# 1/rms at attention's entry put on the products that give k, q and v, with tied logits pairs and later statistics transposes

## The chip, the cores and the metric

The kernel runs on one core of a Trainium2 chip. The metric is the device time of one launch in microseconds (us), as the median of several runs. A core has five engines that run their own queues in order and wait for one another by semaphores: TensorE (PE in the profile, its weight loads PEld), VectorE (DVE), ScalarE (ACT), GpSimd (POOL) and SyncE (SP), which here issues the transfers. Products are gathered in PSUM, eight banks of 512 float32 columns; everything else lies in SBUF.

## The reference, cut to what matters

A trunk of two layers on 1024 positions of width 1024 in float32. Layer 0 mixes by a short gated convolution, layer 1 by differential attention over k and v that are made from the residual stream after layer 0. In each layer a convolution FFN and a gated embedding of the layer (called ple here) follow, and RMS norms stand before and after every part.

```
def rms_norm(x, g):
    return x * rsqrt(mean(x * x, axis=-1) + 1e-6) * g

# layer 1: 8 heads, two maps of 64 each, values of 128
k, v = split(rms_norm(x, g_kv) @ w_kv)
q    = rms_norm(x, g_pre_mix[1]) @ w_q
for each block of 128 queries:
    logits = q . k * 64 ** -0.5 + bias(distance), causal
    probs  = softmax(logits)                        # of both maps, m = 0 and 1
    o      = (probs[m = 0] - lam * probs[m = 1]) @ v
o   = rms_norm(o, g_subln) * (1 - lambda_init)
x   = x + rms_norm(o @ w_o, g_post_mix[1])

# every layer
x   = x + rms_norm(conv_ffn(rms_norm(x, g_pre_ffn)), g_post_ffn)
x   = x + rms_norm(sigmoid(rms_norm(x, g_pre_ple) @ w_gate) * (p @ w_proj), g_post_ple)
```

## The kernel before, in words

Activations lie transposed, channels on the 128 partitions and 512 positions along the free axis. So a half (0 or 1) of the sequence is eight tiles of 128x512, and every stage runs for half 0 and then for half 1. A float32 value is used as two parts in the float32r format, `hi` (a cast, on ScalarE) and `lo` (the value less `hi`, on VectorE, `split`, L249 and L250), and a product takes three passes, hi.hi, lo.hi and hi.lo (`mm3`, L256 to L258). Weights come as 128x1024 pieces (`wr`), get their gain on POOL where the stage asks for it (L159), and are split into `wh` (L162) and `wl` (L165, two of three on VectorE and the third on POOL).

The program is a list of steps. A step loads and splits weights ahead, makes its products, and then gives the background work a number of ticks (`ticks`, two to four for most). The background is a queue of generators, and a tick runs the first of them to its next `yield`. A step's `need` names what must have been made before; where it has not, ticks are spent at once until it has. The order in which each engine gets its instructions is then fixed, before the run, by a planner that takes what it thinks is ready in the order of the program, by its own estimate of durations. On the chip each engine follows that order, ready or not.

The background work between two stages is `gen_post`. It takes the outputs y of a stage with the sum of their squares, `acc`, which has one partial sum for each partition, and makes 1/rms: `mean4` transposes `acc` on TensorE (L307) and sums over the free axis (L309); `rsqrt4` starts on VectorE and ends with ten small instructions on POOL (L291 to L300); `bcast4` spreads the result over the partitions by four transposes (L318) and a copy (L322), which gives `rb`. Then, for each of eight tiles k, y is scaled by it (L430, VectorE), added to x (L432, POOL), and x squared and summed into a new `acc` (L268 on ScalarE, L269 on VectorE). Before attention x is also stored to `xscr` in DRAM (`spill`) for the residual. From the new `acc` comes a second 1/rms by the same chain, and with it the inputs of the next stage: `make_h` multiplies x by `rb` (`hn`, L350) and splits it (L249, L250). In some places (`defer`, half 1 of ple) the inputs are made from x without its 1/rms, and the products of the stage take it on instead: the gates of half 1 are scaled out of PSUM at L710, followed by the sigmoid (L711) and the product with the embedding (L714).

At attention's entry stand, in this order, the eight gate steps of ple for half 1, then k and q of head 0 for half 0, two steps of v, and k and q of head 0 for half 1, ahead of the first attention unit. The k and q products go to the two PSUM tiles `pd` and leave them as `hi` with a factor on ScalarE (L834) and `lo` on VectorE (L835); v leaves by one copy (L865). Its products are those of L861.

Attention has 64 units, a head and a block of 128 queries each. A unit's `softmax` makes the logits of both maps, 64 rows of the array each (L962), three passes for each half of the keys, in the tiles `qk`. A block of the first half keeps both maps in one tile; a block of the second half needs a tile for each map, and there are two tiles in all. L969 adds the bias and takes the minimum of the negated logits, L972 the exponential, L975 to L978 join the maps. `transp` (L988) and `values` (L1003) follow two and three units later. The other projections ("dense" steps) are mixed in between units by `pace`.

## Time and profile before

| | |
|---|---|
| median of 3 runs | 2830.05 us (2828.73 to 2830.48) |
| the profiled execution | 2831.85 us, span 2830.1 us |
| granted TensorE clock, mean | 0.977 |
| busy: TensorE, VectorE, ScalarE, POOL | 2698.0, 1649.8, 1258.5, 815.8 us |

The span is the stretch between the first and the last instruction of one profiled execution; what lies around it is in that execution's own time. The busy times are sums over the span. A granted clock of 1 is 2.4 GHz and one of 0.5 is 1.2 GHz; a value between is a mean over a stretch.

### The profile page before, as it was taken

The numbers are of one execution on the slowest core, as the hardware profiler recorded it, in microseconds if no ns is written. First come the engines' busy times: TensorE is split into PE (matmuls) and PEld (weight loads), VectorE is DVE, ScalarE is ACT, GpSimd is POOL, SyncE is SP. The second block draws the span as 40 slices with busy tenths as digits, with TensorE's granted clock in tenths as the row PEclk, the third lists the DMA queues.
The fourth block names the chain that finished last, engine by engine and source line by source line (L and its number), as shares of the span: only waits on it lengthen the run. The fifth ranks groups of instructions, "written<-read, shape, count | busy, mean of one in ns | idle before, by whom it ended". The sixth has DMA issues, their size and how long they took to land.

```text
span 2830.1 us, 33443 instructions
## 1 busy us (share of the span) xinstructions
PE 2698.0 (95%) x12526; PEld 2186.8 (77%) x12526; DVE 1649.8 (58%) x2171; ACT 1258.5 (44%) x2034; POOL 815.8 (29%) x1037
## 2 busy tenths in 40 slices
PE   8999999999989999884999999998999999999996
PEld 7887877888868888763888888776888887888875
DVE  7446366555485555768554545428755558555577
ACT  5233344444454444533454545534544445444442
POOL 3223142221152211454223222225222115221134
PEclk9999999999999999996999999998999999999998
DMA  4222222222242232232111111352222222222242
GB/s 173 98 96 77 96 83 92 94 97 100 97 136 97 97 105 97 90 104 82 60 45 53 53 53 61 114 206 97 90 97 89 97 97 82 90 97 97 97 141 82
DMA packets 86515, 269.56 MB, mean 95 GB/s; under 512 B 9688, under 2 KB 12032, under 8 KB 86352
## 3 DMA queue, kind: packets, MB, share of 16 engines
q1 hardware_dynamic: 86352, 267.42, 27.8%
q8 instruction: 98, 1.61, 0.2%
q14 instruction: 65, 0.53, 0.1%
HBM read 247.42 MB, written 24.68 MB: 96 GB/s over the span
## 4 chain that ended last, share of the span: by engine, by line
PE 49%; DVE 6%; POOL 1%; issue 1%; ACT 1%; DVEq 0%; ACTq 0%; POOLq 0%
PE ps L257 7%; PE ps L258 7%; PE ps L256 7%; PE qk L962 4%; PE pd L861 3%; PE ps L645 3%; PE ps L644 3%; PE ps L646 3%; PE pd L256 3%; PE pd L257 3%; PE pd L258 3%; PE st L1003 2%; DVE hy L430 2%; PE st L988 1%; DVE acc L269 1%
## 5 line engine op out<-in xcount | busy, mean ns | idle before, releaser
L256 PE MATMUL ps<-hy,wh 128*128 128x512 f32 x1960 | 784.0, 400 | 15.7 <-ACT hy L333 7.5
L257 PE MATMUL ps<-hy,wl 128*128 128x512 f32 x1960 | 784.9, 401 | 14.8 <-DVE wl L165 14.8
L258 PE MATMUL ps<-hy,wh 128*128 128x512 f32 x1960 | 781.3, 399 | 0.0
L165 POOL TENSOR_TENSOR wl<-wr,wh 128x1024 fp32r<-128x1024 f32 x136 | 355.5, 2614 | 1009.3 <-ACT wh L162 997.8
L162 ACT CAST wh<-wr 128x1024 fp32r<-128x1024 f32 x412 | 432.7, 1051 | 321.7 <-PE ps L646 152.4
L257 PEld LDWEIGHTS ps<-hy,wl 128*128 128x128 f32 x1960 | 373.2, 190 | 108.8 <-DVE wl L165 18.3
L165 DVE TENSOR_TENSOR wl<-wr,wh 128x1024 fp32r<-128x1024 f32 x276 | 349.5, 1267 | 184.7 <-ACT wh L162 181.4
L256 PEld LDWEIGHTS ps<-hy,wh 128*128 128x128 f32 x1960 | 372.9, 190 | 108.3 <-ACT hy L333 7.9
L258 PEld LDWEIGHTS ps<-hy,wh 128*128 128x128 f32 x1960 | 372.5, 190 | 90.4 <-DVE hy L334 0.7
L502 DVE SCALAR_TENSOR_TENSOR c<-u,cst,c 128x512 f32<-128x512 f32 x192 | 149.5, 780 | 352.9 <-ACT c L501 348.1
L607 ACT COPY u<-ps 128x512 f32<-128x512 f32 x176 | 103.4, 587 | 409.3 <-PE ps L258 403.5
L644 PE MATMUL ps<-jit,wh 128*128 128x512 f32 x704 | 273.9, 389 | 0.0
L645 PE MATMUL ps<-jit,wl 128*128 128x512 f32 x704 | 273.9, 389 | 0.0
L646 PE MATMUL ps<-jit,wh 128*128 128x512 f32 x704 | 236.2, 389 | 0.0
L250 DVE TENSOR_TENSOR jit<-hid,jit 128x512 fp32r<-128x512 f32 x176 | 166.6, 959 | 95.7 <-ACT jit L249 95.6
L269 DVE TENSOR_TENSOR acc<-acc,sq 128x512 f32<-128x512 f32 x165 | 146.7, 891 | 114.3 <-ACT sq L268 111.0
L644 PEld LDWEIGHTS ps<-jit,wh 128*128 128x128 f32 x704 | 132.2, 188 | 27.6
L645 PEld LDWEIGHTS ps<-jit,wl 128*128 128x128 f32 x704 | 132.2, 188 | 27.4
L646 PEld LDWEIGHTS ps<-jit,wh 128*128 128x128 f32 x704 | 132.2, 188 | 27.4
L249 ACT CAST jit<-hid 128x512 fp32r<-128x512 f32 x176 | 109.4, 622 | 98.6 <-PE ps L646 90.8
L257 PE MATMUL ps<-s,wl 128*128 128x512 f32 (+1 forms) x368 | 143.3, 390 | 10.3 <-DVE wl L165 10.3
L503 DVE SCALAR_TENSOR_TENSOR c<-u,cst,c 128x512 f32<-128x512 f32 x192 | 146.7, 766 | 5.7
(159 smaller groups left out, 3828.5 us busy)
## 6 DMA issues: line engine op xcount, KB each, us to landing
wr<-w_ffn_up SPq DMA_DIRECT2D x176, 512.0 KB, 3.2
wr<-w_ffn_down SPq DMA_DIRECT2D x88, 512.0 KB, 3.2
wr<-w_sc_in SPq DMA_DIRECT2D x48, 512.0 KB, 3.2
wr<-w_ple_gate SPq DMA_DIRECT2D x32, 512.0 KB, 3.3
wr<-w_sc_out SPq DMA_DIRECT2D x16, 512.0 KB, 3.3
wr<-w_o SPq DMA_DIRECT2D x16, 512.0 KB, 3.7
oscr<-oh SPq DMA_DIRECT2D x28, 256.0 KB, 2.0
wr<-w_v SPq DMA_DIRECT2D x10, 512.0 KB, 3.3
```

The lines of the kernel that those rows point to most:

```text
L162: nc.scalar.copy(out=hi[:, :n], in_=raw[:, :n])
L165: eng.tensor_tensor(lo[:, :n], raw[:, :n], hi[:, :n].bitcast(F32), ALU.subtract)
L250: (lo_eng or nc.vector).tensor_tensor(dst_lo, src, dst_hi.bitcast(F32), ALU.subtract)
L256: nc.tensor.matmul(out, whi[:, c], hi, start=(i == 0), stop=False)
L257: nc.tensor.matmul(out, wlo[:, c], hi, start=False, stop=False)
L258: nc.tensor.matmul(out, whi[:, c], lo, start=False, stop=(i == n - 1))
L269: nc.vector.tensor_tensor(acc, acc, t, ALU.add)
L502: nc.vector.scalar_tensor_tensor(c, u_in[:, 1:HT + 1], cst[:, wcol + 1:wcol + 2], c, ALU.mult, ALU.add)
L503: nc.vector.scalar_tensor_tensor(c, u_in[:, 0:HT], cst[:, wcol:wcol + 1], c, ALU.mult, ALU.add)
L644: nc.tensor.matmul(o, hi[:, c], j[:, 0, :], start=(k == 0), stop=False)
L645: nc.tensor.matmul(o, lo[:, c], j[:, 0, :], start=False, stop=False)
L646: nc.tensor.matmul(o, hi[:, c], j[:, 1, :], start=False, stop=(k == NF - 1))
```

## The change

It does three things.

- ple of layer 0 now makes the inputs of k, q and v in the loop that updates x, as `split(hi, lo, xn)` without 1/rms. 1/rms of x is still made (`stat_keep`), and the steps of k, q and v need it: k and q are multiplied by its broadcast (and q by -0.125) on VectorE as they leave PSUM and then split, v by its column form on ScalarE, in two parts of 256 columns. The tile of x is given up after its store inside the loop, no longer after it. The broadcast lies in a third `rb`, no longer in `rk`.
- The logits of the two maps are issued in turn, map 1 first, and `tc.issue_after` ties each to come behind the one before in TensorE's queue. It is an order in that queue and no semaphore; other instructions may come between.
- `lag` puts two ticks before `mean4` and two before `bcast4`, and `behind` ties their transposes to come after the last product of `mm3` (or of the FFN's down step) issued so far.

The tile `oh` of the normed attention output has two buffers where it had three.

```diff
 LEAD = 6
 RATE = 0.75
+LAG_A = 2
+LAG_B = 2
...
         (lo_eng or nc.vector).tensor_tensor(dst_lo, src, dst_hi.bitcast(F32), ALU.subtract)
...
+    last_mm = [None]
+    def behind():
+        return tc.issue_after(last_mm[0]) if last_mm[0] is not None else nullcontext()
     def mm3(out, whi, wlo, pairs, kcols):
...
             nc.tensor.matmul(out, whi[:, c], hi, start=(i == 0), stop=False)
             nc.tensor.matmul(out, wlo[:, c], hi, start=False, stop=False)
-            nc.tensor.matmul(out, whi[:, c], lo, start=False, stop=(i == n - 1))
+            last_mm[0] = nc.tensor.matmul(out, whi[:, c], lo, start=False, stop=(i == n - 1)).ins
...
     def k128(i):
...
     def mean4(sq, nb=4):
...
         m = sb_()
-        for c in range(nb):
-            nc.tensor.transpose(m[:, k128(c)], sq[:, k128(c)], ident)
+        with behind():
+            for c in range(nb):
+                nc.tensor.transpose(m[:, k128(c)], sq[:, k128(c)], ident)
...
     def bcast4(r, keep=False, raw=False):
...
         b = sb_()
-        for c in range(r.shape[1]):
-            nc.tensor.transpose(b[:, k128(c)], r[:, c:c + 1].to_broadcast([P, P]), ident)
+        with behind():
+            for c in range(r.shape[1]):
+                nc.tensor.transpose(b[:, k128(c)], r[:, c:c + 1].to_broadcast([P, P]), ident)
         if raw:
             return b
-        rb = cur[0].tile([P, HT], F32, tag="rk", name=nm("rk"), bufs=2) if keep else wk("rb")
+        rb = cur[0].tile([P, HT], F32, tag="rk", name=nm("rk"), bufs=2) if keep else wk("rb", bufs=3)
...
         return rb
...
-    def stat_keep(sq, key):
+    def lag(n):
+        for _ in range(n):
+            yield
+    def stat_keep(sq, key, on=False):
+        yield from lag(LAG_A)
         v = mean4(sq)
         r = rsqrt4(v, True)
-        yield
-        have["r", key] = (bcast4(r, True), r)
+        yield from lag(LAG_B)
+        have["r", key] = (bcast4(r, not on), r)
...
     def make_hg(x, gname, k, hi, lo):
...
     def stat_r(sq):
+        yield from lag(LAG_A)
         v = mean4(sq)
         r = rsqrt4(v)
-        yield
+        yield from lag(LAG_B)
...
     def make_h(xs, rb, gname, key, alloc, drop=False):
...
         acc = None if last else wk("acc", bufs=3)
         new, hs = [], []
-        if defer:
+        if defer and not spill:
...
                     yield False
                 hi, lo = al(F32R), al(F32R)
-                make_hg(xn, gname, k, hi, lo)
+                if gname is None:
+                    split(hi, lo, xn)
+                else:
+                    make_hg(xn, gname, k, hi, lo)
+                if spill:
+                    hy.free(1)
...
             have[targets[0][1]] = hs
             slots_of[targets[0][1]] = al
-            yield from stat_keep(acc, targets[0][1])
+            yield from stat_keep(acc, targets[0][1], spill)
...
                 slots_of[key] = al
                 have["r", key] = have["r", targets[0][1]]
-            if spill:
-                hy.free(ND)
...
                         nc.tensor.matmul(o, hi[:, c], j[:, 0, :], start=(k == 0), stop=False)
                         nc.tensor.matmul(o, lo[:, c], j[:, 0, :], start=False, stop=False)
-                        nc.tensor.matmul(o, hi[:, c], j[:, 1, :], start=False, stop=(k == NF - 1))
+                        last_mm[0] = nc.tensor.matmul(o, hi[:, c], j[:, 1, :], start=False, stop=(k == NF - 1)).ins
...
                     have[f"y_ple{L}", half] = (ys, acc[0])
                     bg.append(gen_post(half, (f"y_ple{L}", half), f"post_ple{L}", targets, last=(L == 1),
-                                       spill=(L == 0)))
+                                       spill=(L == 0), defer=(L == 0)))
...
                 hi, lo = (pool.tile([P, HT], F32R, tag="kq", name=nm("kq"), bufs=KQ) for _ in range(2))
                 sc = -0.125 if isq else 1.0
-                nc.scalar.activation(hi, p_, AF.Copy, scale=sc)
-                nc.vector.scalar_tensor_tensor(lo, p_, sc, hi.bitcast(F32), ALU.mult, ALU.subtract)
+                t = wk("hn")
+                nc.vector.scalar_tensor_tensor(t, p_, sc, have["r", ("xn", half)][0], ALU.mult, ALU.mult)
+                split(hi, lo, t)
...
                 ensure(hy, 1)
                 v = hy()
-                nc.scalar.copy(out=v, in_=p_)
+                r = have["r", ("xn", half)][1]
+                for j in range(2):
+                    c = slice(j * 256, (j + 1) * 256)
+                    tb = (t2 % 2) * 2 + j
+                    nc.scalar.activation(v[:, c], p_[:, c], AF.Copy, scale=r[:, tb:tb + 1])
...
             w, g = kq(h, isq)
             for i, half in enumerate(halves):
-                step(kq_part(h, isq, half, hold), w if i == 0 or again else None, need=[("xn", half)], g=g,
+                step(kq_part(h, isq, half, hold), w if i == 0 or again else None, need=[("xn", half), ("r", ("xn", half))], g=g,
...
         def v_steps(g, hold, t2s, load):
...
                 step(v_first(hold), a["w_v"][g, 0], ticks=0, g=("kv", 0, 4))
             for i, t2 in enumerate(t2s):
-                step(v_part(g, t2, hold), a["w_v"][g, 1] if load and i == 0 else None, need=[("xn", t2 // 2)], g=("kv", 4, 4),
+                step(v_part(g, t2, hold), a["w_v"][g, 1] if load and i == 0 else None, need=[("xn", t2 // 2), ("r", ("xn", t2 // 2))], g=("kv", 4, 4),
...
                 lg = [ps_.tile([P, S], F32, tag="qk", name=nm("qk"), bufs=2) for _ in range(2)]
             q = qt[h, half]
+            prev = None
...
                 k = kt[h, c]
                 for i, (a_, b_) in enumerate(((0, 0), (0, 1), (1, 0))):
-                    for m in range(2):
+                    for m in (1, 0):
                         r = slice(64 * m, 64 * m + 64)
-                        nc.tensor.matmul(lg[m][:, c * HT:c * HT + ce], q[a_][r, k128(qb)], k[b_][r, 0:ce],
-                                         start=(i == 0), stop=(i == 2))
+                        with tc.issue_after(prev) if prev is not None else nullcontext():
+                            prev = nc.tensor.matmul(lg[m][:, c * HT:c * HT + ce], q[a_][r, k128(qb)], k[b_][r, 0:ce],
+                                                    start=(i == 0), stop=(i == 2)).ins
...
                 hi, lo = hy(F32R), hy(F32R)
             else:
-                hi, lo = (scopes["att"][1].tile([P, HT], F32R, tag="oh", name=nm("oh"), bufs=3) for _ in range(2))
+                hi, lo = (scopes["att"][1].tile([P, HT], F32R, tag="oh", name=nm("oh"), bufs=2) for _ in range(2))
...
             nc.vector.scalar_tensor_tensor(lo, p_, gsub, hi.bitcast(F32), ALU.mult, ALU.subtract)
             if h == NH - 1:
```

## Rows read from the trace of the kernel before

**Rows 1.** The page, busy time, share of the span and instructions of each engine.

```profile
PE 2698.0 (95%) x12526; PEld 2186.8 (77%) x12526; DVE 1649.8 (58%) x2171; ACT 1258.5 (44%) x2034; POOL 815.8 (29%) x1037
```

**Rows 2.** TensorE's waits, whole span: who waited for whom, total, times, longest.

```profile
PE st L307 <- DVE acc L269: 37.6, 7, 19.9
PE ps L257 <- DVE wl L165: 25.1, 12, 5.7
```

**Rows 3.** Stages: busy us of PE, PEld, DVE, ACT, POOL, then clock, DMA share.

```profile
1232.00:1247.00 15.00, 9.53 (x33) 6.94 (x33) 14.45 (x15) 6.63 (x10) 6.89 (x4) 0.89 0.44 154
...
1268.00:1288.00 20.00, 1.10 (x4) 0.60 (x4) 20.00 (x25) 9.34 (x16) 7.08 (x3) 0.57 0.28 100
1288.00:1316.00 28.00, 27.73 (x176) 24.12 (x174) 20.79 (x35) 11.57 (x23) 12.13 (x16) 0.94 0.16 58
1316.00:1341.00 25.00, 1.13 (x5) 0.73 (x5) 20.50 (x31) 8.41 (x17) 16.86 (x18) 0.56 0.30 105
...
1440.00:1560.00 120.00, 120.00 (x746) 100.12 (x744) 58.04 (x136) 55.41 (x126) 33.70 (x68) 1.00 0.15 49
```

**Rows 4.** Timeline around the first k product: start, duration, instruction, times, idle before.

```profile
1268.05 0.39 PE L258 MATMUL ps<-s,wh 128*128 128x512 f32 x1
...
1285.92 1.87 DVE L710 TENSOR_TENSOR hy<-ps,rk 128x512 f32<-128x512 f32 x3
...
1287.34 0.77 PE L256 MATMUL pd<-hy,wh 128*128 128x512 f32 x1 [18.90 <-ACT hy L711]
...
1290.12 3.07 DVE L269 TENSOR_TENSOR acc<-acc,sq 128x512 f32<-128x512 f32 x4
```

**Rows 5.** Timeline of half 1's statistics.

```profile
1307.15 0.56 ACT L322 COPY rb<-st 128x512 f32<-128x512 f32 x1
...
1309.81 11.49 DVE L430 SCALAR_TENSOR_TENSOR hy<-hy,cst,rb 128x512 f32<-128x512 f32 x8
...
1324.24 2.72 DVE L269 TENSOR_TENSOR acc<-acc,sq 128x512 f32<-128x512 f32 x1
...
1335.63 1.12 PE L307 MATMUL st<-ident,acc 128*128 128x128 f32 x4 [19.90 <-DVE acc L269]
1340.99 0.47 PE L318 MATMUL st<-ident,rs_r 128*128 128x128 f32 x1 [4.24 <-POOL rs_r L300]
...
1342.35 0.59 ACT L322 COPY rb<-st 128x512 f32<-128x512 f32 x1 [0.37 <-PE st L318]
...
1359.16 0.60 ACT L834 ACTIVATE kq<-pd 128x512 fp32r<-128x512 f32 x1 [5.12 <-PE pd L258]
```

**Rows 6.** Groups by line and shape: count, busy us, mean ns, idle before.

```profile
L250 DVE TENSOR_TENSOR hy<-hn,hy 128x512 fp32r<-128x512 f32 x76 | 59.9, 800 | 14.4 <-ACT hy L249 13.9
...
L835 DVE SCALAR_TENSOR_TENSOR kq<-pd,kq 128x512 fp32r<-128x512 f32 x32 | 22.0, 688 | 62.2 <-ACT kq L834 61.8
...
L969 DVE CUSTOM_DVE_ANT_0 s<-qk,T 128x1024 f32<-128x1024 f32 x16 | 19.3, 1222 | 1.2 <-PE qk L962 0.8
...
L350 DVE TENSOR_TENSOR hn<-hy,rb 128x512 f32<-128x512 f32 x16 | 12.4, 791 | 5.6 <-ACT rb L322 5.0
...
L710 DVE TENSOR_TENSOR hy<-ps,rk 128x512 f32<-128x512 f32 x13 | 8.6, 680 | 3.6 <-PE ps L258 3.6
```

**Rows 7.** TensorE's timeline, logits of four units (the first shape of a run stands).

```profile
1304.14 0.98 PE L962 MATMUL qk<-kq,kq 64*128 64x256 f32 x12
...
1307.83 1.49 PE L962 MATMUL qk<-kq,kq 64*128 64x384 f32 x12
...
1793.60 1.31 PE L962 MATMUL qk<-kq,kq 64*128 64x512 f32 x6
```

**Rows 8.** Busy time of L962 alone over attention (TensorE, weight loads, clock, DMA).

```profile
1300.00:1840.00 540.00, 109.55 (x576) 72.18 (x576) 0.97 0.19 65
```

**Rows 9.** TensorE's waits for acc from 340 to 1240, and from 1860 to 2740.

```profile
PE st L307 <- DVE acc L269: 12.1, 3, 7.8
...
PE st L307 <- DVE acc L269: 3.5, 2, 2.9
```

More of the change, by code (lines that the diff above doesn't have):

```diff
@@ L2 @@
 from collections import deque
-from contextlib import ExitStack
+from contextlib import ExitStack, nullcontext
 import concourse.bass as bass
@@ L754, in finish @@
             if c == 0:
-                rs = wk("rb")[:, 0:256]
+                rs = wk("rb", bufs=3)[:, 0:256]
                 nc.scalar.copy(out=rs, in_=rb[:, 0:256])
```

## The prediction

> **What bounds the kernel now.** I read the page first: TensorE is busy for 2698.0 us of the span, so an edit counts only where it shortens TensorE's own work or closes one of its gaps [rows 1]. Second, the waits of TensorE, to see which gaps a named producer ends: 37.6 us in seven waits of the statistics transposes L307 for `acc`, 25.1 us in twelve for the lower half of a weight (`wl`), and one of 18.9 us before the first `pd` product [rows 2, 4]. Third, the stages, to tell which engine each is bound by. Around attention's entry TensorE works 1.10 us of the 20 from 1268 and 1.13 us of the 25 from 1316, while VectorE works 20.00 and 20.50 us of them; the granted clock is 0.57 and 0.56 there, so part of those stretches is at 1.2 GHz. In attention proper TensorE works 120.00 of 120.00 us, VectorE 58.04 and ScalarE 55.41 [rows 3]. So the entry is bound by VectorE and the statistics chain, attention by TensorE. What VectorE or ScalarE does in attention is under cover; what TensorE does there is paid in full.
>
> **What the entry waits for.** For half 0, the multiplication by 1/rms (`hn`, L350) and the split (L250) stand in VectorE's queue between the last gates' L710 and L714: the last three L710 run at 1285.92, and the first k product starts at 1287.34, 19 us after the last gate product at 1268.05. The last gates' y is not summed before 1293.2 (L269) [rows 4]. For half 1 the chain of statistics runs twice: from that sum to the broadcast of 1/rms, copied at 1307.15; then eight L430 (11.49 us), the adds on POOL, the sum over x, and L307 at 1335.63, where TensorE has stood 19.90 us; 4.24 us more until 1/rms is back at 1340.99 for L318; only then eight `hn` and eight splits. k of half 1 leaves PSUM at 1359.16 [rows 5].
>
> **The parts, with their cost.**
>
> *Entry.* Removed: 16 `hn` of 791 ns, 12.4 us of VectorE [rows 6]. Moved: 16 pairs of a cast on ScalarE and a split L250 (800 ns) into the loop that updates x, so that k and q need x and not its statistics. The 16 stores to `xscr` are issued where they were, SyncE's queue keeps its order; only the tile is given up sooner. Added: each k and q product is scaled by VectorE out of PSUM (nearest row L710, also PSUM times SBUF, 680 ns), then cast, then split (800), where one scaled copy on ScalarE and L835 (688) did it [rows 6]: about 0.8 us more of VectorE for each of 32, 25 us, under TensorE's 120 of 120 us [rows 3]. Each v leaves in two copies of half width in place of one, on ScalarE, under the same cover. Without that cover the 25 us would be paid: that is rival B.
>
> What is late next is 1/rms of half 1, now needed where k of half 1 leaves PSUM. Behind that multiplication on VectorE stand the softmax minima (L969) and the next `wl`; behind the two `pd` banks stand v, k and q of everything later. When does it come? Without the eight `hn` of half 0 in its way, the last gate's y is summed soon after the last gate product ends (1268.4): L710, sigmoid, L714, square and L269 at 0.6 to 0.8 each, 3.5 us, so 1272 in place of 1293.2 [rows 4]. From there to the copied broadcast took 14 us: 1286. From L430's start to L307 took 25.8 us (1309.8 to 1335.6), with softmax work between; eight splits come in (6.4 us at 0.80, or 11.5 at the 1.44 that an L430 costs beside POOL's adds), and some softmax work can stand elsewhere: I take 28, so 1315. From L307 to the copied broadcast took 7.3 us (1335.63 to 1342.94) [rows 5, 6]: 1323. Meanwhile TensorE has four steps of half 0 and the first units' logits (27.7 us as from 1288 to 1316 [rows 3], of which some 5 are logits, so 5.6 a step), then two steps for k and q of half 1 (11.2) and a few us of the first units' transposes: 42 us from 1268, to 1310. So a wait of some 13 us stays where 43 stood (18.9, 19.9 and 4.2). k of half 1 leaves PSUM at about 1324 in place of 1359, 35 us sooner; the wait that stays leaves the clock low for some us after it, for which I take off 5. **Entry: 30 us**, between 5 (the broadcast is about as late as before, or the splits delay the weights at 1232 to 1247, where VectorE is busy for 14.45 of 15 us [rows 3]) and 45 (no wait left: 43, and the clock).
>
> The Trainium skill speaks against the move (SBUF — State Buffer, "Who interferes with whom"): a VectorE instruction with two SBUF inputs contends with a GpSimd instruction that reads SBUF. The splits have two such inputs and move beside POOL's adds, so by that rule all 16 cost near 1.44 us and the entry would give some 20 to 25 us, not 30; the trace agrees in kind, with an L269 of 2.72 us beside POOL's work and four in 3.07 us elsewhere.
>
> *Tied logits pairs.* The two maps of a head use 64 rows of the array each. Where their products alternate, twelve run in 0.98 us (256 columns) and twelve in 1.49 us (384 and 512, 5,376 columns); where one map's six run alone, they take 1.31 us for 2,304 columns, half of that unit [rows 7]. All 576 keep TensorE busy for 109.55 us [rows 8]. The first four blocks of a head, whose two maps share one tile, already alternate: 0.98 + 1.49 = 2.47 us for each of 8 heads, 19.8 us. The other 32 units have 89.8. They hold 20,736 columns a head (by the code's widths); at the alternating rate (1.49 us for 5,376) that is 5.75 us a head, 46 in all, so 44 us is the most that tying gives, and nothing the least. I take 35: some units alternate already in part, other instructions may come between tied ones, and a pair waits for the later of two tiles. TensorE has no idle time in these stages [rows 3], so its saving is the kernel's.
>
> *Later statistics transposes.* Two ticks before each of the two transposes put L307 and L318 about one step (5.6 us) later in TensorE's queue. Outside entry and end L307 waits 12.1 us before the entry, 7.8 of them at once, and 3.5 us after attention [rows 9]. The 7.8 us is about a step and a half, so most of it should go; for the shorter waits I count nothing, since the tick moves the producer's queue with it. The transposes themselves cost the same. **5 us**, between -8 (the L430 runs shift onto other weights' `wl` waits) and 15 (all of it).
>
> *Nothing:* `oh` with one tile less (its stores have four units, some 28 us, until the next half); the third `rb` (two are held through attention by the halves' 1/rms, and the one left serves the posts there, one at a time).
>
> Sum: 30 + 35 + 5 = 70. The profiled execution took 2831.85 us (span 2830.1), 1.8 above the median of the runs; 2831.85 - 70 = 2761.9, less 1.8 is **2760**.
>
> **Rivals.**
>
> A. *The wait for 1/rms takes the place of the one removed.* k and q of half 1 hold both `pd` banks until the broadcast; if POOL's weight work stands before the ten small rsqrt steps and VectorE's queue holds the sum over x back, the chain keeps its old end. Against: 21 us of the old delay (1272 to 1293.2) is VectorE's backlog at the gates, which goes. Then the entry gives 3: 2787.
>
> B. *Shorter logits don't shorten attention*, because leaving PSUM and softmax set the pace. For: VectorE now scales k and q too. Against: VectorE 58 and ScalarE 55 of 120 us. The pairs then give nothing: 2795. The Trainium skill has this as a rule (TensorEngine Tiling (Array Packing), "PSUM Bottleneck"): tiling speeds TensorE but not the evacuation, which may become the limit.
>
> C. *Slower.* A tied pair waits for the later tile, which the unit before frees only after both its minima (L969, 1.22 us each at 1024 columns [rows 6], behind a queue). Today TensorE starts the first map meanwhile. If the planner places the pair too early, TensorE stands in order behind it. With 32 such units this overtakes the whole gain at 2.2 us a unit (70/32); at 3 us, 96 - 70 gives 2856. Against: L962 is in none of the larger waits of TensorE today, and dense products fill the gaps.
>
> D. *No change:* the order comes out so that each gain is given back elsewhere (the `wl` waits of 25.1 us double, entry as in A): 2830.
>
> **How the numbers follow.** Forecast 0.60 (own range 2738 to 2785), A 0.15, B 0.11, C 0.10, D 0.04. This kernel's measurement tells 0.2% (5.7 us) from no change. Faster: forecast, A and B, 0.86; within 0.2%: D, 0.04; slower: C, 0.10. The range takes in forecast, A and B: from 2734 (entry 42, pairs 42, transposes 12, near their upper ends) to 2800; C and D are left out.
>
> **What would show it.** Right: no gap of TensorE of 19 us between the last gate and the first k; no L350; L962 busy for near 75 us in 576 instructions; L307's waits under 15 us in all. Wrong: a `pd` wait for VectorE's scaling of k of over 25 us; L962 among TensorE's large waits; VectorE busy throughout the entry as before.

## The result and the profile after

The changed kernel takes **2798.24 us** (median of 4, 2797.49 to 2799.38) beside 2830.12 us of the kernel before on the same chip: a ratio of 0.9887 [0.9874, 0.9899], 32 us or 1.1% faster. The forecast was a gain of 70 us. The profiled execution took 2797.83 us (span 2796.0). Two kernels further below had one execution each in a slow state, of 4360.21 and 2938.4 us; their medians are those of the other runs.

New line numbers: mm3 L264 to L266, transposes of the statistics L316 and L328, their sum L318, ten 1/rms steps on POOL L299 to L308, copy of the broadcast L332, gains of weights on POOL L161, `wl` L167, split L252, square and sum L276 and L277, y scaled L446 and added L448, the gates L729, L730 and L733, scaling of k and q L854, v's products L881 and its copies out of PSUM L889, logits L988.

The page's first part and TensorE's longest waits stand against [rows 1, 2].

```profile
PE 2676.2 (96%) x12526; PEld 2168.2 (78%) x12526; DVE 1676.6 (60%) x2187; ACT 1258.1 (45%) x2050; POOL 820.2 (29%) x1037
```

```profile
PE ps L265 <- DVE wl L167: 27.0, 11, 6.3
PE st L328 <- POOL rs_k L308: 23.9, 3, 13.0
PE st L316 <- DVE acc L277: 12.6, 7, 3.3
...
PE pd L266 <- DVE hy L252: 8.3, 3, 5.4
```

The wait of 18.9 us for the gates' last step ahead of the first k product is gone, and the waits for `acc` fell from 37.6 to 12.6 us. A new one has come: 23.9 us for `rs_k`, the end of the ten small steps on POOL. TensorE's own work fell by 21.8 us.

Both kernels issue 12,526 instructions on TensorE, so the start of the n-th shows where time was won (us; the last two columns are experiments below, and the traced execution of the last one took 2756.84 us, the fastest of its kernel):

```
n-th start       before    after    difference   1/rms on VectorE   all three repairs
5000 (ahead)     1194.4   1191.2       -3.2            1192.0            1191.0
5750 (entry)     1394.9   1380.4      -14.5            1370.6            1359.6
8500 (after)     1857.0   1824.9      -32.1            1815.1            1784.2
12526 (last)     2821.0   2787.3      -33.7            2778.3            2746.3
```

Of the 34 us some 3 were won ahead of the entry, 11 in it, 18 in attention and 2 behind it. The entry, by stages as in [rows 3] (the third window is 29 us long, to where TensorE runs on):

```profile
1268.00:1288.00 20.00, 12.66 (x53) 10.39 (x54) 13.26 (x17) 5.82 (x9) 11.56 (x14) 0.83 0.39 133
1288.00:1316.00 28.00, 18.59 (x134) 15.88 (x133) 24.73 (x32) 13.61 (x28) 23.32 (x21) 0.87 0.28 105
1316.00:1345.00 29.00, 14.36 (x54) 10.07 (x53) 18.68 (x30) 9.07 (x18) 12.57 (x15) 0.74 0.20 73
...
1440.00:1560.00 120.00, 120.00 (x771) 98.49 (x771) 71.39 (x157) 58.25 (x135) 38.44 (x82) 1.00 0.16 54
```

TensorE is busy for 45.61 of these first 77 us, where it worked 29.96 of 73 in [rows 3]. In attention proper it stays at 120.00 of 120.00 while VectorE rises from 58.04 to 71.39: the scaling moved there is under cover, as forecast.

Where TensorE stands now, from its timeline (answers to [rows 4, 5]):

```profile
1266.90 0.40 PE L266 MATMUL ps<-s,wh 128*128 128x512 f32 x1
1275.34 1.12 PE L328 MATMUL st<-ident,rs_k 128*128 128x128 f32 x4 [8.04 <-POOL rs_k L308]
1276.10 0.78 PE L264 MATMUL pd<-hy,wh 128*128 128x512 f32 x1
...
1329.84 0.66 PE L316 MATMUL st<-ident,acc 128*128 128x128 f32 x4 [1.37 <-DVE acc L277]
1343.48 0.47 PE L328 MATMUL st<-ident,rs_k 128*128 128x128 f32 x1 [12.98 <-POOL rs_k L308]
```

And what the two long waits wait for, on POOL:

```profile
1268.45 0.20 POOL L299 TENSOR_TENSOR rs_t<-rs_k 128x4 f32<-128x4 f32 x1 [5.25 <-DVE rs_k L287]
1269.35 2.50 POOL L161 TENSOR_TENSOR wr<-wr,cst 128x1024 f32<-128x1024 f32 x1 [0.69 <-DMA wr<-w_v]
1271.81 0.65 POOL L300 TENSOR_TENSOR rs_t<-rs_t,rs_v 128x4 f32<-128x4 f32 x1
...
1275.08 0.20 POOL L308 TENSOR_TENSOR rs_k<-rs_k,rs_t 128x4 f32<-128x4 f32 x1
...
1335.01 0.20 POOL L299 TENSOR_TENSOR rs_t<-rs_k 128x4 f32<-128x4 f32 x1 [1.65 <-DVE rs_k L287]
1335.29 0.20 POOL L300 TENSOR_TENSOR rs_t<-rs_t,rs_v 128x4 f32<-128x4 f32 x1
...
1338.21 1.90 POOL L161 TENSOR_TENSOR wr<-wr,cst 128x1024 f32<-128x1024 f32 x1 [2.15 <-DMA wr<-w_k]
1340.06 0.20 POOL L303 TENSOR_TENSOR rs_t<-rs_k 128x4 f32<-128x4 f32 x1
1340.21 1.90 POOL L161 TENSOR_TENSOR wr<-wr,cst 128x1024 f32<-128x1024 f32 x1
...
1343.22 0.20 POOL L308 TENSOR_TENSOR rs_k<-rs_k,rs_t 128x4 f32<-128x4 f32 x1
```

Ten steps of 0.2 us, issued 0.28 us apart where nothing is between them, would take 2.8 us. They take 6.8 and 8.4 here, because gains of weights stand between them in POOL's order, and these wait for the transfers of the weights (0.69 and 2.15 us) and then run for 1.9 to 2.5 us. VectorE and ScalarE show the rest of both chains, and what the first costs y of half 1:

```profile
1266.62 0.68 DVE L318 TENSOR_REDUCE rs_v<-st 128x4 f32<-128x512 f32 x1
...
1276.49 0.59 ACT L332 COPY rb<-st 128x512 f32<-128x512 f32 x1 [2.49 <-PE st L328]
1276.97 0.64 ACT L730 ACTIVATE hy<-hy 128x512 f32<-128x512 f32 x1
1277.64 2.38 DVE L733 TENSOR_TENSOR hy<-hy,s 128x512 f32<-128x512 f32 x1 [3.25 <-ACT hy L730]
1280.72 0.69 DVE L277 TENSOR_TENSOR acc<-acc,sq 128x512 f32<-128x512 f32 x1 [0.70 <-ACT sq L276]
...
1331.14 3.30 DVE L167 TENSOR_TENSOR wl<-wr,wh 128x1024 fp32r<-128x1024 f32 x1
...
1344.84 0.59 ACT L332 COPY rb<-st 128x512 f32<-128x512 f32 x1 [0.37 <-PE st L328]
1345.46 1.29 DVE L854 SCALAR_TENSOR_TENSOR hn<-pd,rb 128x512 f32<-128x512 f32 x2 [10.54 <-ACT rb L332]
```

The last gate's sigmoid (L730) stands on ScalarE behind the copy of `rb`, which waits for that same 1/rms. So y of half 1 is summed at 1281.4, where the forecast had 1272. POOL is not alone in this: the sum of half 0's statistics (L318) starts on VectorE 7.5 us after its transposes have ended (1259.1), behind the work of the last gates and a `wl`, and in half 1's chain a `wl` of 3.30 us (1331.14) stands on VectorE ahead of the steps for POOL.

### The profile page after: what moved, and what is told of

Read it like the earlier page. It is cut to its first block, busy times and chain, and to the rows that moved or that the text cites. A ratio compares the mean times of both kernels' runs of the same rounds, so it can differ in the third digit from the quotient of the medians.

```text
span 2796.0 us, 33415 instructions
## 1 busy us (share of the span) xinstructions
PE 2676.2 (96%) x12526; PEld 2168.2 (78%) x12526; DVE 1676.6 (60%) x2187; ACT 1258.1 (45%) x2050; POOL 820.2 (29%) x1037
## 4 chain that ended last, share of the span: by engine, by line
PE 47%; DVE 6%; POOL 2%; issue 1%; ACT 1%; DMA 0%; DVEq 0%; SPq 0%; POOLq 0%; ACTq 0%
PE ps L265 7%; PE ps L264 7%; PE ps L266 7%; PE pd L881 3%; PE ps L665 3%; PE ps L663 3%; PE ps L664 3%; PE qk L988 3%; PE pd L264 2%; PE pd L266 2%; PE pd L265 2%; PE st L1029 2%; DVE hy L446 1%; PE st L1014 1%; DVE acc L277 1%
## 5 line engine op out<-in xcount | busy, mean ns | idle before, releaser
L264 PE MATMUL ps<-hy,wh 128*128 128x512 f32 x1960 | 783.2, 400 | 16.4 <-ACT hy L348 8.3
L266 PE MATMUL ps<-hy,wh 128*128 128x512 f32 x1960 | 781.6, 399 | 0.0
L167 POOL TENSOR_TENSOR wl<-wr,wh 128x1024 fp32r<-128x1024 f32 x136 | 355.1, 2611 | 1007.1 <-ACT wh L164 997.8
L264 PEld LDWEIGHTS ps<-hy,wh 128*128 128x128 f32 x1960 | 373.1, 190 | 107.4 <-ACT hy L348 8.6
L266 PEld LDWEIGHTS ps<-hy,wh 128*128 128x128 f32 x1960 | 372.5, 190 | 90.3 <-DVE hy L349 0.8
L167 DVE TENSOR_TENSOR wl<-wr,wh 128x1024 fp32r<-128x1024 f32 x276 | 348.2, 1262 | 155.5 <-ACT wh L164 154.9
L252 DVE TENSOR_TENSOR jit<-hid,jit 128x512 fp32r<-128x512 f32 x176 | 168.2, 968 | 98.0 <-ACT jit L251 97.9
L277 DVE TENSOR_TENSOR acc<-acc,sq 128x512 f32<-128x512 f32 x165 | 146.1, 889 | 112.0 <-ACT sq L276 110.0
```

Of the source, the lines that this page charges most:

```text
L167: eng.tensor_tensor(lo[:, :n], raw[:, :n], hi[:, :n].bitcast(F32), ALU.subtract)
L252: (lo_eng or nc.vector).tensor_tensor(dst_lo, src, dst_hi.bitcast(F32), ALU.subtract)
L264: nc.tensor.matmul(out, whi[:, c], hi, start=(i == 0), stop=False)
L266: last_mm[0] = nc.tensor.matmul(out, whi[:, c], lo, start=False, stop=(i == n - 1)).ins
L277: nc.vector.tensor_tensor(acc, acc, t, ALU.add)
```

## The experiments

Times are medians; "before" beside experiments 1 and 2 was 2829.73 us, beside 3 to 5 2829.28, beside 6 2830.24. The changed kernel was not measured again beside them: taken from each group's own "before", the gains over it in experiments 2 to 5 come out 0.4 to 0.8 us smaller than the differences of medians given here.

**1. The three parts alone.** The entry alone: the changed kernel with the old order of logits and transposes.

```diff
-LAG_A = 2
-LAG_B = 2
+LAG_A = 0
+LAG_B = 1
...
-        return tc.issue_after(last_mm[0]) if last_mm[0] is not None else nullcontext()
+        return nullcontext()
...
-                    for m in (1, 0):
+                    for m in range(2):
...
-                        with tc.issue_after(prev) if prev is not None else nullcontext():
```

> The entry's part alone: 1/rms on the products, without the tie between the logits products and with no tick or tie on the statistics transposes. The parts add up (read from the trace of after, by the start of TensorE's n-th product against before): the entry gave 12 us, so 2818 (2814 to 2822). Rival, the later transposes are what lets the entry close: alone it leaves L307's transposes of half 1 ahead of useful products as before, and gives under 4 us: 2826 or more. My forecast's size, 30 us: 2800.

Measured: 2814.62 us, ratio 0.9947 [0.9935, 0.996], a gain of 15.1, inside the range expected; the rival (under 4 us) falls.

The tied pairs alone, on the kernel before:

```diff
-                    for m in range(2):
+                    for m in (1, 0):
...
-                        nc.tensor.matmul(lg[m][:, c * HT:c * HT + ce], q[a_][r, k128(qb)], k[b_][r, 0:ce],
-                                         start=(i == 0), stop=(i == 2))
+                        with tc.issue_after(prev) if prev is not None else nullcontext():
+                            prev = nc.tensor.matmul(lg[m][:, c * HT:c * HT + ce], q[a_][r, k128(qb)], k[b_][r, 0:ce],
+                                                    start=(i == 0), stop=(i == 2)).ins
```

> The tied logits pairs alone, on the kernel before. The parts add up: about 21 us in attention, 2809 (2805 to 2813). Rival, the shorter logits only pay while the rest moves too, because waits for softmax come up: 2818 or more. My forecast's size, 35 us: 2795.

Measured: 2812.26 us, 0.9938 [0.9924, 0.9951], a gain of 17.5, again inside the range.

The later transposes alone, on the kernel before:

```diff
+LAG_A = 2
+LAG_B = 2
...
+        with behind():
+            for c in range(nb):
+                nc.tensor.transpose(m[:, k128(c)], sq[:, k128(c)], ident)
...
+        yield from lag(LAG_A)
         v = mean4(sq)
         r = rsqrt4(v)
-        yield
+        yield from lag(LAG_B)
```

> The two ticks and the ties of the statistics transposes alone, on the kernel before. The parts add up: 3 us won at 792 and given back at 1200, so 2827 to 2831. My forecast's size, 5 us: 2825. Rival, the ticks work at the entry: more than 10 us, under 2820.

Measured: 2827.2 us, 0.9989 [0.9981, 0.9998], a gain of 2.5; the rival of more than 10 us falls. The three gains add to 35.1, against 31.9 together: the parts stand nearly by themselves, and each of the three is about half of its term (30, 35, 5).

**2. The entry: POOL's steps.** The changed kernel, with the ten 1/rms steps after layer 0's ple on VectorE.

```diff
-        r = rsqrt4(v, True)
+        r = rsqrt4(v, True, fast=on)
...
-    def stat_r(sq):
+    def stat_r(sq, on=False):
...
-        r = rsqrt4(v)
+        r = rsqrt4(v, fast=on)
...
-        rb = yield from stat_r(yacc)
+        rb = yield from stat_r(yacc, spill)
```

> After, with the rsqrt of the posts at attention's entry (both halves of ple in layer 0, both statistics) made wholly on VectorE, as the kernel's end already does, so that none of its steps stands on POOL behind the weight gains (L161) that wait for a weight's transfer. If POOL's queue is what kept 1/rms late, the wait of 8.0 us at 1267 and most of the 13.0 us at 1330 go, and 4 us before half 1's L446: 2798 - 15 = 2783 (2778 to 2789). Rival, VectorE's chain decides (L446 and the sum over x, 31 us from 1298 to 1329): 2794 to 2799, and L328 waits as long, for VectorE.

Measured: 2789.05 us, 0.9854 [0.9841, 0.9868], 9.2 us less than the changed kernel, where 15 were expected; the rival (4 us at most) falls. TensorE's two waits, in its timeline, fall from 8.04 and 12.98 us:

```profile
1273.54 1.08 PE L328 MATMUL st<-ident,rs_k 128*128 128x128 f32 x4 [4.40 <-DVE rs_k L297]
...
1334.20 0.47 PE L328 MATMUL st<-ident,rs_k 128*128 128x128 f32 x1 [4.50 <-DVE rs_k L297]
```

The table above puts all of the 9 us between the 5000th and the 5750th instruction. The steps' own pace is the smaller part: eight steps 0.20 us apart on VectorE against ten 0.28 us apart on POOL differ by 1.2 us a chain, at most 3.6 us for the three chains that follow one another here. The rest, over half of the 9.2, is left to the place in the queue.

**3. The pairs: a lone first product and broken runs.** In the changed kernel's TensorE order the logits stand in 95 runs (97 in the kernel before); 29 of these are a single product (10 before). A unit's first product (map 1) needs one tile, and the planner places it where that comes free; the eleven that are tied behind it need the other tile too. The changed kernel's timeline:

```profile
1692.15 0.28 PE L881 MATMUL pd<-wl,hy 128*128 128x256 f32 x1
1692.36 0.50 PE L988 MATMUL qk<-kq,kq 64*128 64x512 f32 x1
1692.78 0.50 PE L881 MATMUL pd<-wh,hy 128*128 128x256 f32 x2
```

The lone product holds TensorE from 1692.36 to 1692.78, 0.42 us, where a run of twelve, six of 512 and six of 256 columns, takes 1.25 us (below). Two edits were tried. One gives the products a higher priority with the planner; the other claims both tiles, by a store into one column of each, before the first product.

```diff
+                for t in lg:
+                    nc.vector.memset(t[:, 0:1], 0.0)
...
-                        with tc.issue_after(prev) if prev is not None else nullcontext():
+                        with tc.high_priority(offset=200), tc.issue_after(prev) if prev is not None else nullcontext():
```

With both lines:

> The changed kernel, with the products of a unit kept together: a one-column store claims both qk tiles before the unit's first product, and the planner gives the products a higher priority, so that a unit's twelve (or six, eight) come as one run in TensorE's order: 56 runs, 40 of them of twelve, none of one, where the changed kernel has 95 runs, 29 of them of a single product that took the first free tile alone. Theory 'loose ties' (the pairs lack their missing gain because the first product stands alone and other work splits the runs): the products' own share of TensorE falls from 79.5 us (from the first start of a run to the next other start) to 66 to 70, and the time from 2798.2 to about 2787 (2784 to 2791). Rival 'both tiles must be waited for' (case C of the forecast on a small scale: TensorE stands before a run until the later tile is free): the share falls as much, but waits for the minima (L995 to qk) of 5 us and more come up, and the time is 2794 to 2802.

Measured: **2777.25 us**, 0.9811 [0.9798, 0.9824], 21.0 us less than the changed kernel, and more than expected. A unit in its timeline (two lines more in the file, so L990), and the busy time of all logits in the changed kernel and in this one, to be held against [rows 8]:

```profile
1630.48 0.83 PE L1031 MATMUL st<-hy,at 128*128 128x128 f32 x6
1631.24 1.31 PE L990 MATMUL qk<-kq,kq 64*128 64x512 f32 x12
1632.49 1.38 PE L1031 MATMUL st<-hy,at 128*128 128x128 f32 x10
```

```profile
1285.00:1800.00 515.00, 85.70 (x576) 52.56 (x576) 0.97 0.19 64
```

```profile
1290.00:1800.00 510.00, 68.15 (x576) 46.94 (x576) 0.97 0.22 75
```

From 109.55 us before to 85.70 with the change, and to 68.15 with whole runs. By starts, the measure of the expectation, the share fell from 79.5 to 64.2 us. Waits of the logits for their tiles don't appear among TensorE's larger waits, so the rival falls. Part of what a broken run costs lies beside it. In the changed kernel from 1345 to 1800, the start-to-start medians tell it:

```
128-row product of 512 columns, next a 128-row one       234 ns
the same, next a logits product                          327 ns
the same, just behind a logits product                   338 ns
first pair of logits products of a run, 512 columns      336 ns
a pair inside a run                                      231 ns
last pair of a run                                       327 ns
```

So a run costs about 0.1 us on the product ahead of it, 0.1 on its own first pair, 0.1 on its last, and 0.1 on the product behind it. The Trainium skill has a rule for it (TensorEngine Tiling (Array Packing), "Key Properties"): a change of tiling mode drains TensorE. These rows agree and give the price. It is not any change of product: from transposes of 128 columns to a 512-column product, both on 128 rows, the last transpose takes 28 ns in place of 109 and the product 318 in place of 234, nothing in sum. 39 runs fewer at 0.4 us are 16 us. A lone product also leaves two products of its unit without a partner, each some 0.1 us longer than as half of a pair: 29 times, 6 us more. That comes to 22 us, and 21.0 were measured.

The higher priority alone, without the claim:

> As the run before without the store that claims the tiles: only the higher priority. The first product of most units still stands alone (28 runs of one, 28 of eleven), the other breaks are fewer (85 runs in place of 95). Theory 'loose ties': about a third of the gain of the run before, 2793 to 2797; if the lone first products alone cost the missing gain, no change from the changed kernel, 2797 to 2799; if they cost nothing, it is as fast as the run before.

Measured: 2792.08 us, 0.9866 [0.9853, 0.9879], 6.2 us less than the changed kernel, 0.3 of what both lines give. The order has ten runs fewer, 4 us at 0.4 each (where the other 2 come from was not traced), and 28 lone products, nearly as before. So most of the missing gain hung on the lone first product: without the claim a unit isn't one run. The claim without the priority was not run.

**4. Both repairs together.** The diffs of 2 and 3 in one kernel.

> The changed kernel with both repairs: the ten 1/rms steps at the entry on VectorE, and the units' products kept together. If the two causes are separate, the gains add: 9.2 us (as run) and that of the products kept together, 11 by theory, so 2778 (2775 to 2782). If the entry's earlier units collide with the waiting for both tiles, less than the sum: 2783 to 2790.

Measured: 2767.4 us, 0.978 [0.9766, 0.9793]. The number expected held only the 11 us that theory gave the pairs. With their measured 21.0, the sum is 2798.2 - 9.2 - 21.0 = 2768.0, and 2767.4 was measured: the two causes are separate.

**5. The adds beside VectorE.** With the 1/rms steps on VectorE (experiment 2), the entry's adds of y to x leave POOL as well.

```diff
-            nc.gpsimd.tensor_tensor(xn, xs[k], ys[k], ALU.add)
+            (nc.vector if spill else nc.gpsimd).tensor_tensor(xn, xs[k], ys[k], ALU.add)
```

> The changed kernel with the 1/rms steps on VectorE, and the entry's adds of y to x too (L448, sixteen of 128x512, on POOL until now). Theory 'the shared port costs': at half 1 the eight L446 took 10.9 us in two groups and three splits 1.75 to 2.83 us each beside POOL's adds (0.68 alone), some 8 us more than alone; moved adds cost VectorE 5.4 us of their own but end as soon as the product, so that x is complete 3 to 6 us sooner: 2783 to 2787. Rival 'VectorE is the bound at the entry and the slowing is hidden': the adds lengthen its queue by 5.4 us a half, 2791 to 2796. No change: 2788 to 2790.

Measured: 2783.15 us, 0.9835 [0.9822, 0.9848], 5.9 us less than experiment 2, as the theory had it, though VectorE, which was busy for 27.69 of the 28 us from 1288 to 1316 in experiment 2, was given 16 adds of 0.68 us more. Most of what the adds had cost was not on the splits but on the sixteen scalings of y (L446), from 21.9 us in sum to 14.0 (experiment 2, then this one: minimum, median and maximum in ns):

```profile
L446 DVE SCALAR_TENSOR_TENSOR hy<-hy,cst,rb x16: 746/1776/2384, 1220.7 to 1300.3; 128x512 f32<-128x512 f32 x16
```

```profile
L446 DVE SCALAR_TENSOR_TENSOR hy<-hy,cst,rb x16: 740/746/2855, 1220.7 to 1296.6; 128x512 f32<-128x512 f32 x16
```

The splits of x fell from a mean of 1052 ns to 848. Only a few of the sixteen are slow: four in experiment 2 (1.75 to 2.83 us), two of them beside POOL's adds and two beside its weights, and two here (1.77 and 2.30), beside weights. The others take 0.68 us in both kernels. So of the three slow splits of half 1 that the expectation put beside the adds, one was.

```profile
L252 DVE TENSOR_TENSOR hy<-hy,hy 128x512 fp32r<-128x512 f32 x16 | 16.8, 1052 | 0.0
```

```profile
L252 DVE TENSOR_TENSOR hy<-hy,hy 128x512 fp32r<-128x512 f32 x16 | 13.4, 848 | 0.0
```

The transposes of half 1's `acc` came at 1318.95, where experiment 2 had 1327.23. But TensorE then stood 9.69 us for `rs_k` (4.50 there), and before that 8.54 us for a bank of `pd` that v had to leave (L889): on ScalarE v's copies stand behind the squares and casts of half 1's x, and the first of these waits 4.68 us for VectorE's adds.

```profile
1303.63 0.80 PE L264 MATMUL pd<-hy,wh 128*128 128x512 f32 x1 [8.54 <-ACT hy L889]
...
1329.30 0.44 PE L328 MATMUL st<-ident,rs_k 128*128 128x128 f32 x1 [9.69 <-DVE rs_k L297]
```

The small steps met POOL's weights instead. VectorE and POOL in this kernel:

```profile
1320.52 3.30 POOL L167 TENSOR_TENSOR wl<-wr,wh 128x1024 fp32r<-128x1024 f32 x1 [7.91 <-ACT wh L164]
1321.53 2.31 DVE L320 TENSOR_SCALAR rs_v<-rs_v 128x4 f32<-128x4 f32 x1
...
1324.99 1.90 POOL L161 TENSOR_TENSOR wr<-wr,cst 128x1024 f32<-128x1024 f32 x1 [1.18 <-DMA wr<-w_k]
1325.07 1.84 DVE L294 TENSOR_TENSOR rs_t<-rs_t,rs_v 128x4 f32<-128x4 f32 x1
...
1327.24 1.90 POOL L161 TENSOR_TENSOR wr<-wr,cst 128x1024 f32<-128x1024 f32 x1 [0.35 <-DMA wr<-w_q]
1327.34 1.81 DVE L297 SCALAR_TENSOR_TENSOR rs_k<-rs_u,rs_k 128x4 f32<-128x4 f32 x1
```

**6. All three repairs, and the ticks once more.** The diffs of 2, 3 and 5 together:

> All three repairs in one kernel: 1/rms steps of the entry on VectorE, the entry's adds to x on VectorE, the units' products kept together. The causes lie in different places, so by addition 2767.4 less the 5.9 us that the adds gave: 2761.5 (2758 to 2765), which is 68 to 69 us below the kernel before and about what the forecast took the change to give. If the kept-together products of the first units delay the statistics at the entry, part is lost: 2765 to 2770.

Measured: **2761.12 us**, 0.9758 [0.9745, 0.977], 69 us less than before and the fastest kernel of the study. The causes are separate again. TensorE still waits 10.4 us for `rs_k` and 7.8 for v's bank at the entry. The same kernel without the ticks:

```diff
-LAG_A = 2
-LAG_B = 2
+LAG_A = 0
+LAG_B = 0
```

> The kernel with all three repairs, without the two ticks before each statistics transpose (both set to 0, the ties of the transposes kept). Theory 'the ticks are worth their 2.5 us, and what is left waits for the weights' lower halves and 1/rms in their place': 2 to 4 us slower than with the ticks, 2764 to 2766. Rival 'with the entry repaired the ticks cost the entry what they win elsewhere': the same within 1 us. If the ticks do more at the entry than elsewhere, over 6 us slower.

Measured: 2763.5 us, 0.9764 [0.9751, 0.9777]. 2.4 us slower by the medians, the size of the theory, but its runs (2763.05 to 2764.12) lie within those of the kernel with ticks (2756.84 to 2764.4): not told apart.

## Why the prediction was wrong

The direction held, and each part won time by what it was meant to remove; the sizes did not hold. The steps that failed are the terms of the sum: entry 30, pairs 35, transposes 5. They measured 15.1, 17.5 and 2.5 alone. That 2798.24 lies inside the recorded range of 2734 to 2800 is luck: the range reaches so far up for rival B, which is not what happened.

**Entry, 30 forecast, 15.1 measured alone.** What was forecast to go has gone: `hn` is no longer there, the first k product runs 9.2 us behind the last gate (1266.90 to 1276.10) where it was 19, and VectorE's added work in attention is covered. The failed step is "a wait of some 13 us stays where 43 stood". From 1262 to 1346 TensorE's waits fell from 43.2 us only to 32.2, most of it in two lines:

```profile
PE st L328 <- POOL rs_k L308: 21.0, 2, 13.0
PE pd L266 <- DVE hy L252: 8.3, 3, 5.4
```

One wait of 13 us (12.98) did stay, but two stand beside it that had no term. The first k products don't need half 0's 1/rms, but TensorE takes its queue in order, and they stood for 8.04 us behind the transposes (L328) that do. And k of half 1 needs the splits of half 1's x (L252), for which it waited 8.3 us. The forecast had TensorE through with that k at 1310, though by its own working x was summed only at 1315, its splits not long before.

1/rms of half 1 was late too, copied by 1345.43 in place of the forecast 1323. y was summed at 1281.4 in place of 1272. From there to the copied broadcast of its 1/rms 14.5 us passed, about the 14 forecast (L446 began at 1298.0, 2 us behind it). From L446 to the transposes of x's `acc` 31.8 us passed in place of 28 (the forecast's 1286 and 28 give 1314, not its 1315). From these to the copied broadcast 15.6 us passed in place of 7.3. The first and the last, some 18 of the 22 us, hold a chain of 1/rms whose POOL steps stand among weights (4.0 and 5.6 us over their 2.8) and whose VectorE steps stand behind gates and a `wl`. Rival A named this mechanism ("POOL's weight work stands before the ten small rsqrt steps"), but as a case in which the entry gives only 3. It was a matter of degree: moving the steps off POOL gave 9 us (experiment 2, their own pace included).

POOL's adds took another 6 (experiment 5), and what fell most with them was the scalings of y, which the forecast had left as they were (11.49 us for eight). With both repaired the entry is worth 15.1 + 9.2 + 5.9 = 30.2, the forecast size. This agreement is partly chance, since the forecast's own ways to it were other ones. The Trainium skill's rule in the prediction (SBUF — State Buffer, "Who interferes with whom") put the 16 splits near 1.44 us and the entry at 20 to 25. In the changed kernel twelve of the 16 took 0.68 to 0.74 us and four 1.76 to 2.83, each of these four beside a POOL instruction: one beside an add, three beside weights. So the trace agrees with the rule in kind; what failed is that all 16 would meet the adds, which were over when most of the splits began.

**Pairs, 35 forecast, 17.5 measured alone.** The step that failed is "I take 35" out of 44: it went by the busy time of whole runs. The bound of 44 was sound: whole runs took the logits' busy time to 68.15 us, 41.4 below before. But the ties are only an order; they neither hold the first product back nor keep other work out. The forecast saw this ("other instructions may come between tied ones") and put it into a discount of 9 us without a price; a run costs 0.4 us and a lone product 0.42. Rival B fell: from 1350 to 1790 no wait of TensorE on evacuation sums to more than 1.0 us in this kernel and 2.6 with whole runs. The rule of the Trainium skill on evacuation (TensorEngine Tiling (Array Packing), "PSUM Bottleneck") did not come to bear; the page speaks of a fourfold speedup, and two maps side by side give at most a twofold one. Rival C fell too, since even with both tiles claimed first, the wait for them stayed out of TensorE's larger waits.

**Transposes, 5 forecast, 2.5 measured alone.** From 340 to 1240 the waits for `acc` fell from 12.1 to 4.9 us, and the longest from 7.8 to 3.3, as forecast. But other waits came up in the same stretch of the changed kernel:

```profile
PE ps L265 <- DVE wl L167: 8.7, 4, 2.8
PE st L316 <- DVE acc L277: 4.9, 3, 3.3
PE st L328 <- POOL rs_k L308: 2.8, 1, 2.8
...
PE st L328 <- POOL rs_r L308: 1.1, 1, 1.1
```

Before, these were 6.4, 12.1, 1.5 and none. Counting nothing for the shorter waits was the error: of the 7.2 us won at `acc`, 4.7 returned there, and 2.5 were left. In the kernel with the transposes alone, `acc` fell by 6.0 us and the others rose by 5.5 in this stretch, so the waits alone don't tell where its 2.5 us lie. Rival D did this to one part, not to the whole.

**What the forecast's signs said.** No gap of 19 us: held. No `hn`: held. L988 busy near 75: 85.70, the clearest sign of the missing half. `acc` waits under 15 us: 12.6. The sign of a wrong entry, a wait of over 25 us on the scaling of k, did not show as such; 21.0 us stood at L328, one step earlier in the chain. VectorE was no longer busy throughout the entry (13.26 of the first 20 us, 24.73 of the next 28).

What stays open: whether weights' gains away from POOL would win the last 4.5 to 9.7 us of `rs_k`, and v's copies ahead of the work on x the wait at L889. Neither was tried.

## What to carry to other kernels

Before counting a stall as gone, follow the chain that ends next through each engine's queue, and look for large work between its small steps that waits for a transfer: ten steps of 0.2 us took 8.4. An order tie doesn't make a run: here the products on half the rows came near their rate only when every tile was claimed before the first product and their priority was raised. Cost each change between 64 and 128 rows on TensorE as a term of its own.

## What was not expected of the hardware

- Changing between products of 64 and of 128 rows cost TensorE some 0.4 us for each run of 64-row ones: 0.1 us on the product ahead, 0.1 on the first pair of the run, 0.1 on the last, 0.1 on the product behind. A lone 64-row product of 512 columns held TensorE for 0.42 us, a pair of them inside a run for 0.23.
- A VectorE instruction on 128x4 values, 0.16 to 0.17 us as a rule, took 1.81 to 2.31 us when a POOL instruction on 128x1024 ran beside it, ending with or just after it (1327.34 + 1.81 against 1327.24 + 1.90). In these three rows the loss goes not by the size of the VectorE instruction but by what is left of POOL's.
